# mLSTM gate rows: GpSimd fills the scan's mask, another order of scans and exponential, transposes two ticks later

## The chip, the cores and the metric

The kernel runs on one core of a Trainium2 chip. Its engines are TensorE (PE, with its weight loads, PEld), VectorE (DVE), ScalarE (ACT), GpSimd (POOL) and SyncE, whose queue (SP) issues most DMAs. The metric is the device time of one execution in microseconds; smaller is better. The kernel before takes 2407.82 us (median of three runs, 2406.78 to 2409.0).

## The reference

One inference step of a two-layer encoder, for a prompt of 1024 rows and a sample of 32 rows, all in fp32 with width 1024. Layer 0 is an mLSTM mixer with 4 heads, and an MLP; layer 1 is chunk-band attention and an MLP. The change lies in the mixer, in the two gates of each head:

```
gates = (proj[..., 2 * QK_A + 2 * V_A:] + b_if)
ig = gates[..., :NH_A]
lf = log_sigmoid(gates[..., NH_A:])
# in each chunk:
b = cumsum(lf)                              # restarts at each chunk
dmat = b[t] - b[s] + ig[s]                  # causal, else -inf
m_t = max(b + m, max over s of dmat)        # running maximum
wts = exp(dmat - m_t);  a = exp(b + m - m_t)
h = num / max(abs(den), exp(-m_t))
```

So out of two short rows per head (one value per token) come the sums b, the running maxima m, their differences, and exp(-m), which all later work of the mixer needs, some of it by token along the partitions.

## The kernel before

Tokens are worked on in three blocks of 384, 384 and 288 (TBS). Each fp32 weight and operand is split into a high and a low part (lines 89 and 90: a cast on ScalarE, a subtraction on VectorE), and each product is three matmuls per 128 rows of depth (lines 118 to 120), so a block of a projection is 24 matmuls.

The mixer runs in this order. `v_first` makes the values of head 0 and, in 8 extra columns, the gates, which stand by token along the partitions in `g64`. Then `gate_rows` (lines 526 to 581) works the gates out, and `qk_proj(0, tick)` makes the queries (j = 0) and keys (j = 1) of head 0: three blocks each, a copy of each block by ScalarE (line 600), then on VectorE a convolution of four instructions (lines 608 and 611), and a SiLU in three pieces that goes back and forth between ScalarE (459 to 461, 616) and VectorE (462, 617). For heads 1 to 3, `qk_proj` and `v_proj` follow, and beside them runs `mlstm` of the head before, in steps: `scores` (the product of keys and queries, line 668, and the weights W, line 666), `values` and `heads` (transposes, line 738).

`gate_rows` first turns the gates so that each head is one partition and the tokens lie along the free dimension (transposes, line 542). The rows are 4 partitions by 1056 elements: `ig`, `fr` (forget gate), `tt` (its log-sigmoid, `neglogsig`), `mr` (maxima), `br` (sums) and `rr` (br - mr); br and rr are the two halves of one tile, and `stk` is a tile of 36 partitions, whose first four take ig - br and whose last four take exp(-m). Two scans with add and max make mr (547, 549). A third scan makes br: it multiplies the running value by a mask that is 1, and 0 at each chunk's start, and adds tt. The mask is written into `fr` by two VectorE memsets (551, 552), since fr is no longer needed then. Then come the difference into stk (554), rr (555), its DMA to DRAM, the decay rows (557 to 562) with their DMAs, then -m cut at 80 (569) and its exponential into stk (570), and two small outputs by DMA (571, 572).

At its `yield GATE` the generator stops. It goes on when the flow's ticks have used up GATE: `qk_proj` ticks once after the first and after the second block of the queries, once after their convolution and SiLU, and likewise for the keys. With GATE = 3.0 the rest follows in the program text after the queries' convolution, ahead of the first key block. The rest is nine transposes of stk into `ae_ps` (577), their copies to `ae` (579, 581) and a GpSimd memset (580). `ae` is read by W in `scores`. In between, `ada_l0` (lines 279 and 281) does modulation sums of layer 0 on VectorE in pieces, by ticks too.

The program text isn't the order on the engines. A planner fixes at build time, for each engine, the order in which its instructions stand, from its own estimate of when each is ready, earlier text first among those that are. On the chip each engine then works in that order and waits where an operand is late. So in the trace line 569 stands ahead of line 558 on VectorE. Only the MLPs and the attention have TensorE's order written out.

Of the kernel before, what the change touches and what calls it, by code (L numbers as in the profile page):

```python
# [10 lines left out]
AF = mybir.ActivationFunctionType  # L11
ALU = mybir.AluOpType
# [15 lines left out]
CH = 128  # L28
# [47 lines left out]
def trunk_kernel(ctx: ExitStack, tc: tile.TileContext, a, o):  # L76
    nc = tc.nc
# [101 lines left out]
    def tpt(name):  # L179
        return pa.tile([P, 512], F32, tag="tp", name=name, bufs=2)  # L180
# [269 lines left out]
            pt2[:, 0:16].rearrange("p (q b) -> p q b", q=4)[:, :, :, None].broadcast_to([P, 4, 4, 2]), op=ALU.add)  # L450


    GATE = 3.0
    ADA_C = (2.0, 3.0, 2.0)
    w_in = a["w_in_a"][0]

    def neglogsig(dst, src):

        nc.scalar.activation(dst, src, AF.Abs)
        nc.scalar.activation(dst, dst, AF.Exp, scale=-1.0)  # L460
        nc.scalar.activation(dst, dst, AF.Ln, bias=1.0)
        nc.vector.scalar_tensor_tensor(dst, src, 0.0, dst, op0=ALU.min, op1=ALU.subtract)
# [63 lines left out]
    def gate_rows():  # L526
        nonlocal ae

        def row(name):
            return A.tile([P, YL], F32, tag="y", name=name, bufs=4)[0:NH, :T]  # L530
        ig, fr, tt, mr = row("ig"), row("fr"), row("tt"), row("mr")
        rc = A.tile([P, 2, T], F32, tag="rc", name="rc_rows", bufs=1)
        br, rr = rc[0:NH, 0], rc[0:NH, 1]
        stk = A.tile([P, KC, T], F32, tag="G", name="stk")[0:36, 0]
        nc.gpsimd.memset(stk, 0.0)
        for t0 in range(0, NT, 4):
            ts = list(range(t0, min(NT, t0 + 4)))
            ps = tpt(f"gt_{t0}")
            n = 0
            for t in ts:  # L540
                m = P if t < NT - 1 else TS
                nc.tensor.transpose(ps[:36, n:n + m], g64[:m, t, :], ident[:m, :m])
                n += m
            nc.scalar.activation(ig[:, t0 * P:t0 * P + n], ps[0:NH, :n], AF.Identity, bias=bif[0:4])
            nc.scalar.activation(fr[:, t0 * P:t0 * P + n], ps[32:32 + NH, :n], AF.Identity, bias=bif[32:36])
        neglogsig(tt, fr)
        nc.vector.tensor_tensor_scan(out=mr[:, :TP], data0=tt[:, :TP], data1=ig[:, :TP], initial=0.0,
                                     op0=ALU.add, op1=ALU.max)
        nc.vector.tensor_tensor_scan(out=mr[:, TP:], data0=tt[:, TP:], data1=ig[:, TP:], initial=m0[:, 0:1],
                                     op0=ALU.add, op1=ALU.max)  # L550
        nc.vector.memset(fr, 1.0)
        nc.vector.memset(fr[:, ::CH], 0.0)
        nc.vector.tensor_tensor_scan(out=br, data0=fr, data1=tt, initial=0.0, op0=ALU.mult, op1=ALU.add)
        nc.vector.tensor_sub(stk[0:NH], ig, br)
        nc.vector.tensor_sub(rr, br, mr)
        nc.sync.dma_start(rc_d[0], rr)
        nc.scalar.copy(fr[:, :CH], rr[:, :CH])
        nc.vector.tensor_add(fr[:, CH:TP].rearrange("p (c t) -> p c t", t=CH),
                             rr[:, CH:TP].rearrange("p (c t) -> p c t", t=CH),
                             mr[:, CH - 1:TP - CH:CH][:, :, None].broadcast_to([NH, NCK - 1, CH]))  # L560
        nc.vector.tensor_scalar_add(fr[:, TP:], rr[:, TP:], m0[:, 0:1])
        nc.scalar.activation(fr, fr, AF.Exp)
        nc.sync.dma_start(rc_d[1], fr)
        al = A.tile([NH, NT], F32, name="al")
        nc.vector.tensor_copy(al[:, :NCK], fr[:, CH - 1:TP:CH])
        nc.vector.tensor_copy(al[:, NCK:], fr[:, T - 1:])
        nc.sync.dma_start(al_d, al)
        nc.sync.dma_start(albc, al_d[None].broadcast_to([P, NH, NT]))
        nc.vector.tensor_scalar(tt, mr, -1.0, 80.0, op0=ALU.mult, op1=ALU.min)
        nc.scalar.activation(stk[32:36], tt, AF.Exp)  # L570
        nc.sync.dma_start(o["m_p"].rearrange("a b h -> (a b h)")[:, None], mr[:, TP - 1:TP])
        nc.sync.dma_start(o["m_s"].rearrange("a b h -> (a b h)")[:, None], mr[:, T - 1:T])
        yield GATE
        ps = tpt("ae_ps")
        for t in range(NT):
            m = P if t < NT - 1 else TS
            nc.tensor.transpose(ps[:m, t * 36:(t + 1) * 36], stk[:, t * P:t * P + m], ident[:36, :36])
        ae = A.tile([P, NT, 36], F32, tag="ga", name="ae", bufs=1)
        nc.vector.tensor_copy(ae[:, :NT - 1], ps[:, :(NT - 1) * 36].rearrange("p (t c) -> p t c", c=36))
        nc.gpsimd.memset(ae[:, NT - 1], 0.0)  # L580
        nc.vector.tensor_copy(ae[:TS, NT - 1], ps[:TS, (NT - 1) * 36:NT * 36])
# [221 lines left out]
    for t0, n in TBS:  # L803
        nc.sync.dma_start(xsp[0][:, :, t0:t0 + n], xt[:, :, t0:t0 + n])
    flow.finish()
    gates = flow.add(gate_rows(), now=True)

    def ada_l0():
# [1425 lines left out]
```

## Time and profile before

| what | value |
|---|---|
| median of three runs | 2407.82 us (2406.78 to 2409.0) |
| the profiled execution | 2407.76 us, of which its span is 2405.9 us |
| TensorE busy | 2341.9 us |
| VectorE busy | 1935.6 us |
| ScalarE busy | 1204.7 us |
| GpSimd busy | 168.7 us |
| mean granted clock of TensorE | 0.995 |

A row of the timeline reads: start and duration in us, engine, line, operation, output <- inputs, shape, count, and in square brackets how long the engine had been idle before it and what released it. A row of the waits reads: who, for whom, us in total, times, the longest. A row of busy time by stretch has the stretch, its length, busy us and count of each engine, the granted clock, and the share and rate of the DMA engines. Times are from the start of the span; 1.9 us of the profiled execution lie outside it.

### The profile page before, as it was taken

Reading aid. Unit: us, or ns where it says so; the run is one execution under the profiler, and the core shown is the slowest. Engines: PE = TensorE matmul, PEld = TensorE weight load, DVE = VectorE, ACT = ScalarE, POOL = GpSimd, SP = SyncE. Lnnn points to the kernel's source line nnn. Section 1 sums busy time; section 2 is a strip of 40 time slices with the busy share of each in tenths; the row PEclk is TensorE's granted clock in tenths of the full one; section 3 lists DMA queues with packets and bytes.
Section 4 is the critical chain, followed back from the end, with each engine's and each line's share of the span. In section 5 each row is a group of like instructions: output and inputs, shape, how many; then the busy total and the mean of one; then the engine's idle time right before and its main releaser. Section 6 shows DMA issues by size and latency. Waiting matters only on the chain. (4 is left out here: it accounts for less than half of the span.)

```text
span 2405.9 us, 44188 instructions
## 1 busy us (share of the span) xinstructions
PE 2341.9 (97%) x17180; PEld 2249.5 (93%) x17180; DVE 1935.6 (80%) x3904; ACT 1204.7 (50%) x2452; POOL 168.7 (7%) x322
## 2 busy tenths in 40 slices
PE   7999999999999999999999999999999999899997
PEld 4999999999999999999999987789999999899997
DVE  4888766778788789989888776756998889888777
ACT  4665557278656630101148467773776777222212
POOL 0211100000000000000000224420000000000003
PEclk9999999999999999999999999999999999999999
DMA  8343222526566896675512330051486779976642
GB/s 302 120 137 98 77 91 64 177 93 203 186 197 199 287 341 230 245 268 212 178 61 84 82 93 1 10 140 58 168 278 210 260 280 335 356 257 234 225 148 73
DMA packets 284277, 424.64 MB, mean 177 GB/s; under 512 B 15384, under 2 KB 205228, under 8 KB 278948
## 3 DMA queue, kind: packets, MB, share of 16 engines
q1 hardware_dynamic: 279540, 390.95, 48.3%
q10 hardware_dynamic: 4528, 30.87, 3.2%
q8 instruction: 135, 2.21, 0.4%
q14 instruction: 74, 0.61, 0.1%
HBM read 305.96 MB, written 118.17 MB: 176 GB/s over the span
## 5 line engine op out<-in xcount | busy, mean ns | idle before, releaser
L1133 DVE SCALAR_TENSOR_TENSOR ACX<-dn,ada,ACX 128x264 f32<-128x264 f32 (+6 forms) x664 | 281.7, 447 | 84.3 <-PE dn L1503 41.1
L1503 PE MATMUL dn<-fx,wf_d 128*128 128x264 f32 x2016 | 254.1, 285 | 6.4 <-DVE ACX L1133 4.0
L1503 PEld LDWEIGHTS dn<-fx,wf_d 128*128 128x128 f32 x2016 | 248.8, 188 | 8.7 <-DVE ACX L1133 2.7
L89 ACT CAST w_dn<-raw_dn 128x1024 fp32r<-128x1024 f32 x36 | 37.7, 1051 | 283.3 <-DVE aw L279 124.5
L118 PE MATMUL dn<-hs,w_dn 128*128 128x384 f32 (+2 forms) x512 | 161.3, 315 | 0.0
L119 PE MATMUL dn<-hs,w_dn 128*128 128x384 f32 (+2 forms) x512 | 160.9, 315 | 0.0
L120 PE MATMUL dn<-hs,w_dn 128*128 128x384 f32 (+2 forms) x512 | 156.3, 314 | 1.3 <-DVE w_dn L90 1.3
L1368 PE MATMUL up<-TF,wf_u 128*128 128x264 f32 x1056 | 143.2, 285 | 2.8 <-ACT H L1371 2.8
L1368 PE MATMUL up<-U,wf_u 128*128 128x264 f32 x1056 | 139.8, 285 | 1.1 <-DVE H L1374 0.6
L1368 PE MATMUL up<-u,wf_u 128*128 128x264 f32 x1056 | 139.6, 284 | 1.3 <-ACT wf_u L89 0.7
L279 DVE SCALAR_TENSOR_TENSOR aw<-radw,cs,aw 128x512 f32<-128x512 f32 x196 | 139.5, 743 | 0.8 <-DMA radw<-in_w_ada_dram 0.8
L1368 PEld LDWEIGHTS up<-TF,wf_u 128*128 128x128 f32 x1056 | 134.4, 188 | 3.8 <-ACT H L1371 3.7
L1368 PEld LDWEIGHTS up<-U,wf_u 128*128 128x128 f32 x1056 | 132.9, 188 | 1.9 <-DVE H L1374 1.2
L1368 PEld LDWEIGHTS up<-u,wf_u 128*128 128x128 f32 x1056 | 132.9, 188 | 1.9 <-ACT wf_u L89 0.9
L118 PE MATMUL dn<-U,w_dn 128*128 128x384 f32 (+2 forms) x416 | 129.2, 311 | 0.3 <-DVE ada L304 0.3
L119 PE MATMUL dn<-U,w_dn 128*128 128x384 f32 (+2 forms) x416 | 129.3, 312 | 0.0
L120 PE MATMUL dn<-U,w_dn 128*128 128x384 f32 (+2 forms) x416 | 125.8, 313 | 1.0 <-DVE w_dn L90 0.9
L1876 ACT ACTIVATE p<-p,mx 128x576 f32<-128x576 f32 (+9 forms) x132 | 86.6, 657 | 27.4 <-DVE mx L1873 25.1
L120 PEld LDWEIGHTS dn<-hs,w_dn 128*128 128x128 f32 x512 | 95.9, 188 | 2.0 <-DVE w_dn L90 1.8
L90 DVE TENSOR_TENSOR HL<-H,HL 128x1056 fp32r<-128x1056 f32 x64 | 80.3, 1254 | 21.6 <-ACT HL L89 21.5
L119 PEld LDWEIGHTS dn<-hs,w_dn 128*128 128x128 f32 x512 | 96.4, 188 | 0.0
L118 PEld LDWEIGHTS dn<-hs,w_dn 128*128 128x128 f32 x512 | 96.3, 188 | 0.1
(419 smaller groups left out, 7102.0 us busy)
## 6 DMA issues: line engine op xcount, KB each, us to landing
hpl<-HL SPq DMA_DIRECT2D x144, 264.0 KB
rdn_u<-in_w_up_dram SPq DMA_DIRECT2D x64, 512.0 KB
hd<-HL SPq DMA_DIRECT2D x28, 1056.0 KB
fx<-hd SPq DMA_DIRECT2D x50, 528.0 KB
radw<-in_w_ada_dram SPq DMA_DIRECT2D x24, 1024.0 KB
hd<-HM SPq DMA_DIRECT2D x28, 792.0 KB
raw_up<-in_w_up_dram SPq DMA_DIRECT2D x40, 512.0 KB
raw_dn<-in_w_down_dram SPq DMA_DIRECT2D x36, 512.0 KB
```

What stands on the lines that cost most here:

```text
L89: nc.scalar.copy(dst_h, src)
L90: (eng or nc.vector).tensor_sub(dst_l, src, dst_h.bitcast(F32))
L118: nc.tensor.matmul(ps, wh, mov(0, k), start=(k == 0), stop=False)
L119: nc.tensor.matmul(ps, wh, mov(1, k), start=False, stop=False)
L120: nc.tensor.matmul(ps, wl, mov(0, k), start=False, stop=(k == nk - 1))
L279: nc.vector.scalar_tensor_tensor(acc[cnd], raw[:, k], sc, acc[cnd], op0=ALU.mult, op1=ALU.add)
L1133: nc.vector.scalar_tensor_tensor(xs, ps[:, off + o:off + o + mm_], gate[:, fc, cnd:cnd + 1], xs, op0=ALU.mult, op1=ALU.add)
L1368: nc.tensor.matmul(p, self.ws[w][:, wl, k], moving(f, tp, xl, k), start=first and k + n_ == 0, stop=k == 3 and n_ == 2, skip_group_check=n ...
L1503: nc.tensor.matmul(p, ws[w][:, wl, k], t[:, s0, xl], start=first and k + n_ == 0, stop=k == kg - 1 and n_ == 2, skip_group_check=not first)
L1876: nc.scalar.activation(z, z, AF.Exp, bias=mx[:, 0:1], scale=-1.0, accum_out=mx[:, 1:2])
```

## The change

The mask for the scan of the forget gates is written by two GpSimd memsets into `rr`, which is free until the difference is put there, at the start of `gate_rows`; the two VectorE memsets into `fr` go. The scan into br comes first of the three scans. The cut of -m and its exponential into stk come right behind the scans, ahead of the differences, in place of after the decay rows. GATE is 5.0 in place of 3.0: the transposes stand in the program text after the second key block, ahead of the third.

```
-    GATE = 3.0
+    GATE = 5.0
...
         nc.gpsimd.memset(stk, 0.0)
+        nc.gpsimd.memset(rr, 1.0)
+        nc.gpsimd.memset(rr[:, ::CH], 0.0)
...
         neglogsig(tt, fr)
+        nc.vector.tensor_tensor_scan(out=br, data0=rr, data1=tt, initial=0.0, op0=ALU.mult, op1=ALU.add)
         nc.vector.tensor_tensor_scan(out=mr[:, :TP], data0=tt[:, :TP], data1=ig[:, :TP], initial=0.0,
                                      op0=ALU.add, op1=ALU.max)
         nc.vector.tensor_tensor_scan(out=mr[:, TP:], data0=tt[:, TP:], data1=ig[:, TP:], initial=m0[:, 0:1],
                                      op0=ALU.add, op1=ALU.max)
-        nc.vector.memset(fr, 1.0)
-        nc.vector.memset(fr[:, ::CH], 0.0)
-        nc.vector.tensor_tensor_scan(out=br, data0=fr, data1=tt, initial=0.0, op0=ALU.mult, op1=ALU.add)
+        nc.vector.tensor_scalar(tt, mr, -1.0, 80.0, op0=ALU.mult, op1=ALU.min)
+        nc.scalar.activation(stk[32:36], tt, AF.Exp)
         nc.vector.tensor_sub(stk[0:NH], ig, br)
         nc.vector.tensor_sub(rr, br, mr)
         nc.sync.dma_start(rc_d[0], rr)
...
         nc.sync.dma_start(albc, al_d[None].broadcast_to([P, NH, NT]))
-        nc.vector.tensor_scalar(tt, mr, -1.0, 80.0, op0=ALU.mult, op1=ALU.min)
-        nc.scalar.activation(stk[32:36], tt, AF.Exp)
         nc.sync.dma_start(o["m_p"].rearrange("a b h -> (a b h)")[:, None], mr[:, TP - 1:TP])
```

More of the change, by code (lines that the diff above doesn't have):

```diff
@@ L450, in ada_first @@
             pt2[:, 0:16].rearrange("p (q b) -> p q b", q=4)[:, :, :, None].broadcast_to([P, 4, 4, 2]), op=ALU.add)
-    GATE = 3.0
+    GATE = 5.0
     ADA_C = (2.0, 3.0, 2.0)
@@ L535, in gate_rows @@
         nc.gpsimd.memset(stk, 0.0)
+        nc.gpsimd.memset(rr, 1.0)
+        nc.gpsimd.memset(rr[:, ::CH], 0.0)
         for t0 in range(0, NT, 4):
@@ L546, in gate_rows @@
         neglogsig(tt, fr)
+        nc.vector.tensor_tensor_scan(out=br, data0=rr, data1=tt, initial=0.0, op0=ALU.mult, op1=ALU.add)
         nc.vector.tensor_tensor_scan(out=mr[:, :TP], data0=tt[:, :TP], data1=ig[:, :TP], initial=0.0,
@@ L550, in gate_rows @@
                                      op0=ALU.add, op1=ALU.max)
-        nc.vector.memset(fr, 1.0)
-        nc.vector.memset(fr[:, ::CH], 0.0)
-        nc.vector.tensor_tensor_scan(out=br, data0=fr, data1=tt, initial=0.0, op0=ALU.mult, op1=ALU.add)
+        nc.vector.tensor_scalar(tt, mr, -1.0, 80.0, op0=ALU.mult, op1=ALU.min)
+        nc.scalar.activation(stk[32:36], tt, AF.Exp)
         nc.vector.tensor_sub(stk[0:NH], ig, br)
@@ L568, in gate_rows @@
         nc.sync.dma_start(albc, al_d[None].broadcast_to([P, NH, NT]))
-        nc.vector.tensor_scalar(tt, mr, -1.0, 80.0, op0=ALU.mult, op1=ALU.min)
-        nc.scalar.activation(stk[32:36], tt, AF.Exp)
         nc.sync.dma_start(o["m_p"].rearrange("a b h -> (a b h)")[:, None], mr[:, TP - 1:TP])
```

## The prediction

> **What bounds the kernel now.** I read the page first, then the list of waits of TensorE, then TensorE's order of work around the change, then VectorE, ScalarE and GpSimd over the same stretch.
>
> ```profile
> span 2405.9 us, 44188 instructions
> PE 2341.9 (97%) x17180; PEld 2249.5 (93%) x17180; DVE 1935.6 (80%) x3904; ACT 1204.7 (50%) x2452; POOL 168.7 (7%) x322
> ```
>
> TensorE is busy for 2341.9 of 2405.9 us, so the kernel gains only where TensorE stops waiting or runs faster. The change touches one such place. From the list of TensorE's waits:
>
> ```profile
> PE hT L738 <- ACT hn L731: 3.7, 4, 1.3
> PE ae_ps L577 <- ACT stk L570: 2.4, 1, 2.4
> ```
>
> The nine transposes of the gate rows (L577) wait once, for 2.4 us, for ScalarE's exponential L570. The order on TensorE, first the second key block's start, its last matmul before the wait, and the transposes:
>
> ```profile
> 86.56 0.34 PE L118 MATMUL qk<-U,w_qk 128*128 128x384 f32 x1
> ...
> 89.20 0.33 PE L118 MATMUL qk<-U,w_qk 128*128 128x384 f32 x1
> 91.96 0.72 PE L577 MATMUL ae_ps<-ident,stk 36*128 36x36 f32 x9 [2.43 <-ACT stk L570]
> ```
>
> A block has 8 x 3 = 24 matmuls. From 86.56 to 89.20 at 0.176 us each, 15 have gone by, so the transposes stand behind the sixteenth of the second key block. That is not their place in the program text (ahead of the first key block): the planner that fixes the order at build time put them where its own estimate has the rows ready, and it was about 2.4 us too early.
>
> The wait costs more than its length. Busy time by stretch (columns: length, TensorE, weight loads, VectorE, ScalarE, GpSimd, each with its count, then granted TensorE clock, DMA share, GB/s):
>
> ```profile
> 89.50:92.00 2.50, 0.07 (x2) 0.04 (x1) 2.50 (x5) 1.45 (x3) 0.20 (x2) 1.00 0.05 10
> 92.00:96.00 4.00, 4.00 (x22) 3.94 (x23) 3.92 (x8) 1.86 (x3) 0.68 (x1) 0.64 0.07 12
> 96.00:99.00 3.00, 3.00 (x22) 3.00 (x22) 3.00 (x4) 1.05 (x1) 0.59 (x2) 0.92 0.94 331
> 99.00:113.00 14.00, 14.00 (x87) 14.00 (x87) 12.19 (x18) 10.92 (x30) 3.91 (x7) 1.00 0.17 47
> 113.00:141.00 28.00, 27.72 (x190) 26.30 (x189) 27.93 (x64) 20.08 (x57) 4.24 (x15) 1.00 0.19 61
> ```
>
> Behind the wait the clock is 0.64 for 4 us and 0.92 for 3: 4 x 0.36 + 3 x 0.08 = 1.7 us more. Without the wait TensorE has 2.43 + 1.7 = 4.1 us to gain. The second thing to see is the last row: from 113 to 141 VectorE is busy for 27.93 of 28 us beside a TensorE at 27.72. In that stage two engines run neck and neck.
>
> **Which waits cost the clock.** Three more rows bound it: a wait at the query projection, the stretch behind it, and the stretch that holds the longest wait at the heads, the 1.3 us of the list above:
>
> ```profile
> 1255.86 0.44 PE L120 MATMUL q<-U,w_q 128*128 128x384 f32 x1 [2.88 <-DVE w_q L90]
> ...
> 220.00:225.00 5.00, 4.01 (x27) 2.79 (x28) 1.97 (x7) 3.75 (x11) 0.19 (x2) 1.00 0.57 183
> 1255.00:1260.00 5.00, 4.14 (x16) 4.13 (x17) 5.00 (x7) 0.99 (x2) 0.00 (x0) 0.70 0.51 156
> ```
>
> A wait of 2.88 us is followed by clock 0.70, as the one of 2.43 us by 0.64, while around the 1.3 us the clock stays at 1.00. So the price sets in somewhere between 1.3 and 2.43 us. [...]
>
> **The change part by part.** The gate rows now, on VectorE, then ScalarE, GpSimd and the SP queue, then who uses what follows:
>
> ```profile
> 79.56 2.27 DVE L547 TENSOR_TENSOR_SCAN mr<-tt,ig 4x1024 f32<-4x1024 f32 x1
> 81.76 0.25 DVE L549 TENSOR_TENSOR_SCAN mr<-tt,m,ig 4x32 f32<-4x32 f32 x1
> 82.18 0.94 DVE L551 MEMSET fr<- 4x1056 f32 x1 [0.17 <-issue]
> 83.05 1.15 DVE L90 TENSOR_TENSOR w_qk<-raw_qk,w_qk 128x1024 fp32r<-128x1024 f32 x1
> 84.14 0.73 DVE L279 SCALAR_TENSOR_TENSOR ada_acc<-ada_room,cs,ada_acc 128x512 f32<-128x512 f32 x1
> ...
> 84.80 2.34 DVE L553 TENSOR_TENSOR_SCAN rc_rows<-fr,tt 4x1056 f32<-4x1056 f32 x1
> 87.06 0.72 DVE L279 SCALAR_TENSOR_TENSOR ada_acc<-ada_room,cs,ada_acc 128x512 f32<-128x512 f32 x1
> 87.71 1.24 DVE L554 TENSOR_TENSOR stk<-ig,rc_rows 4x1056 f32<-4x1056 f32 x1
> 88.88 1.24 DVE L555 TENSOR_TENSOR rc_rows<-rc_rows,mr 4x1056 f32<-4x1056 f32 x1
> 90.05 0.69 DVE L569 TENSOR_SCALAR tt<-mr 4x1056 f32<-4x1056 f32 x1
> ...
> 92.71 0.46 DVE L579 COPY ae<-ae_ps 128x288 f32<-128x288 f32 x1
> ...
> 90.82 1.08 ACT L570 ACTIVATE stk<-tt 4x1056 f32<-4x1056 f32 x1 [0.37 <-DVE tt L569]
> ...
> 97.44 1.05 ACT L89 CAST w_v<-raw_v 128x1024 fp32r<-128x1024 f32 x1 [1.77 <-PE qk L120]
> ...
> 104.07 0.97 ACT L666 ACTIVATE W<-rc,ae 128x128 f32<-128x128 f32 x3
> ...
> 66.99 0.97 POOL L535 MEMSET stk<- 36x1056 f32 x1 [20.10 <-DVE w_qk L90]
> ...
> 81.86 0.29 SPq L571 DMA_DIRECT2D out_dram<-mr  x1
> ...
> 84.22 0.40 SPq L96 DMA_DIRECT2D raw_v<-in_w_in_a_dram  x1
> ```
>
> *The mask's memsets leave VectorE.* From the end of L549 (82.01) to L90's start (83.05) that is 1.0 us of a full engine. GpSimd takes over a 4x1056 and a 9-element memset. No row shows them; the nearest is 0.97 us for 36x1056, so about 1.1 us for both, behind the memset at 66.99, done by 69.1. The scan that reads them starts at 79.6 at the earliest: 10 us of cover, cost nothing, and +1.1 us on the chain if that cover were gone. [...]
>
> *The rows are ready earlier.* I keep the three interleaved instructions (1.09 + 0.66 + 0.65 us by their starts). New order from 79.56: scan of the forget gates 2.26, L547 and L549 2.45, the three others 2.4, L569 0.62: it ends at about 87.3. Then the exponential (1.08) and L554 (1.24) run side by side, to about 88.6, against 91.90 now. ScalarE is idle there; behind the exponential in its queue stand only the copies of key blocks.
>
> *The transposes move.* GATE 5.0 puts them behind the second key block's 24 matmuls, which end at 86.56 + 24 x 0.176 = 90.8. The rows are ready 2.2 us before that. The wait goes, unless the planner delays the rows by more than those 2.2 us. Their two copies (L579, 0.46 us, and a short one) and GpSimd's memset of the last row move with them; the first reader is L666 at 104.07, over 10 us later: nothing. L571 and L572 follow L549, now some 2.3 us later, in SP's queue ahead of the load at 84.22; its cast runs at 97.44 and waits for TensorE anyway: nothing.
>
> **Who takes part of it back.** TensorE runs ahead of VectorE by what it gains more. Rows of VectorE, ScalarE, TensorE and the waits of the first head's scores:
>
> ```profile
> 95.79 1.32 DVE L611 SCALAR_TENSOR_TENSOR y<-qkp,pt,y 128x1059 f32<-128x1059 f32 x1
> ...
> 101.38 0.97 DVE L462 SCALAR_TENSOR_TENSOR sl<-y,sl 128x353 f32<-128x353 f32 x2 [1.81 <-ACT sl L461]
> ...
> 112.96 0.95 DVE L617 SCALAR_TENSOR_TENSOR y<-y,sl 128x353 f32<-128x353 f32 x2
> ...
> 99.02 0.37 ACT L600 COPY qkp<-qk 128x256 f32<-128x256 f32 x1 [0.54 <-PE qk L120]
> 99.29 0.89 ACT L459 ACTIVATE sl<-y 128x353 f32<-128x353 f32 x2
> ...
> 113.53 0.49 PE L668 MATMUL S<-y,y 128*128 128x128 f32 x2
> ...
> PEld S L668 <- DVE y L617: 0.5, 1, 0.5
> ...
> 141.22 1.59 ACT L731 ACTIVATE hn<-hn,sm 128x256 f32<-128x256 f32 x3 [0.35 <-DVE sm L727]
> ```
>
> The first scores (L668 at 113.53) already wait for the keys that L617 finishes at 112.96 plus: there is no slack. So their new time is VectorE's. VectorE gains the 1.0 us of memset. It also gains the 1.81 us that it idled at 101.38: ScalarE's L459 was late only because it stood behind the copy L600, and that behind TensorE. With TensorE 4.1 us earlier, L459 can start when the convolution ends (97.1 less 1.0), 3 us earlier, and its result comes before VectorE has done its own work. Together 2.8 us. From there to 141 VectorE has no idle time left to give, and the first heads (L731 at 141.22) hang on it. I therefore take 2.8 us, with 4.1 - 2.8 = 1.3 us of new waiting at L668. The bounds: 4.1 us if the planner sets the scores later, 1.0 us if VectorE keeps its gap.
>
> Sum against the profiled execution, 2407.76 us (1.9 us more than its span): 2407.8 - 2.8 = 2405.0. The median of the runs, 2407.82, is the same to 0.1. Later stages follow TensorE, as its 97% say, so I carry the 2.8 us to the end.
>
> **The rivals.**
> 1. *TensorE keeps all of it.* Order on both engines is planned anew, and scores, set a few matmuls later, find their keys. For it: TensorE has v and key blocks to fill with. Against it: the planner knew nothing of the wait, and sees VectorE's work shorter by the memset, which moves scores earlier if anything. 2407.8 - 4.1 = 2403.7; with heads' waits (3.7 us in all) partly gone too, down to 2400.
> 2. *The wait at L668 costs the clock.* If the scores are planned 1 us earlier, for the shorter VectorE chain, the wait is 1.3 + 1.0 = 2.3 us, next to the 2.43 that cost 1.7. Then 2405.0 + 1.7 = 2406.7.
> 3. *Slower: the heads' transposes L738.* They wait four times, at most 1.3 us, at full clock. Being ahead by 1.3 us there too, TensorE would wait up to 2.6 and pay 1.7 of clock: 3.0 us a head. One head cancels the forecast's gain; two make -2.8 + 6.0 = +3.2, 2411.0. It decides from a wait of about 2.4 us on. Against it: each wait absorbs the lead, so the next head should not find it again.
> 4. *The change doesn't do what it says.* The rows are later than 90.8, because the planner lets convolution or modulation work of VectorE go first. Then the old wait stays and only the memset's 1.0 us is gained: 2406.8.
>
> **How the numbers follow.** Forecast 0.43, rival 1 0.22, rival 2 0.16, rival 3 0.11, rival 4 0.08. The likeliest gives 2405.0. The range goes from the lower part of rival 1, 2401, to a first head lost in rival 3 with some rest, 2409.5; beyond it lie rival 3's two heads and the best of rival 1. A measurement of this kernel can tell about 0.2% from no change, 4.8 us: faster means below 2403.0, slower above 2412.6. Rival 1 only just misses that by its own sum and passes it with one or two head waits less: faster 0.16. Slower needs three heads of rival 3: 0.07. Same 0.77.
>
> **What would show it.** Right: the nine transposes stand behind a whole second key block without a wait, and no stretch between 85 and 105 has a clock below 1.00; the exponential starts near 87.4, beside the subtraction into stk; GpSimd's memsets end before 70; VectorE's gap before L462 near 98 is gone; the first scores start near 110.7 behind a wait of about 1.3 us, at full clock. Wrong: a wait still named at the transposes (rival 4); no new wait at the scores and TensorE 4 us early at 141 (rival 1); a clock below 1.00 behind the scores (rival 2) or behind the heads (rival 3). A time outside 2401 to 2409.5 with these steps in place would mean that the planner moved something far from the gate rows, which no step here covers.

## The result: slower by about 3.4 us

The changed kernel takes 2410.73 us, the median of 22 runs (2407.52 to 2417.05); the kernel before, run beside it, 2407.36 us, the median of 22 (2404.82 to 2411.8). The ratio is 1.0014, 95% interval 1.0008 to 1.0019: slower by about 3.4 us, where 2.8 us less was forecast. By the bound of 0.2% it is no change. The profiled execution of the kernel after took 2410.11 us, 1.8 us more than its span.

First the page of the kernel after, then its list of TensorE's waits (the rows that answer to those of before), each in its own fence:

```profile
span 2408.3 us, 44186 instructions
...
PE 2341.6 (97%) x17180; PEld 2249.8 (93%) x17180; DVE 1932.9 (80%) x3902; ACT 1205.1 (50%) x2452; POOL 168.3 (7%) x324
```

```profile
PE S L668 <- DVE y L617: 4.4, 1, 4.4
PE hT L738 <- ACT hn L731: 4.0, 5, 1.4
```

VectorE's busy time is 2.7 us less, TensorE's the same to 0.3 us, and the span 2.4 us longer. The wait at the transposes (2.4 us) is gone from the list, and one of 4.4 us at the first scores is new. The order on TensorE in the kernel after:

```profile
91.21 0.34 PE L120 MATMUL qk<-U,w_qk 128*128 128x384 f32 x1
91.47 0.72 PE L577 MATMUL ae_ps<-ident,stk 36*128 36x36 f32 x9
...
114.92 0.58 PE L668 MATMUL S<-y,y 128*128 128x128 f32 x1 [4.42 <-DVE y L617]
```

And its busy time by stretch (length, TensorE, weight loads, VectorE, ScalarE, GpSimd, granted clock, DMA share, GB/s):

```profile
85.00:105.00 20.00, 20.00 (x128) 19.69 (x127) 17.94 (x27) 11.11 (x25) 8.04 (x10) 1.00 0.26 85
105.00:110.00 5.00, 5.00 (x35) 5.00 (x34) 5.00 (x5) 0.00 (x0) 0.00 (x0) 1.00 0.43 112
110.00:115.00 5.00, 0.58 (x4) 0.26 (x2) 5.00 (x10) 4.59 (x13) 0.34 (x1) 0.91 0.07 22
115.00:121.00 6.00, 6.00 (x20) 5.63 (x21) 5.23 (x10) 3.00 (x8) 0.29 (x2) 0.50 0.00 0
```

From 85 to 110 TensorE works without a break at clock 1.00, transposes included. Then it waits from 110.5 to 114.92, and behind the wait the clock is 0.50 for 6 us: 6 x 0.5 = 3.0 us more. The new place costs 4.42 + 3.0 = 7.4 us where the old one cost 4.1. The difference, 3.3 us, is close to the 3.4 of the medians. That it fits so well is partly luck: the two profiled spans lie only 2.4 us apart, and the price in clock differs between waits of the same length (last section).

What makes it wait is VectorE. Its rows in the kernel after, from the gate rows to the keys (L617 at 114.35):

```profile
84.80 1.22 DVE L556 TENSOR_TENSOR stk<-ig,rc_rows 4x1056 f32<-4x1056 f32 x1
85.95 0.69 DVE L554 TENSOR_SCALAR tt<-mr 4x1056 f32<-4x1056 f32 x1
...
97.11 0.94 DVE L462 SCALAR_TENSOR_TENSOR sl<-y,sl 128x353 f32<-128x353 f32 x2
97.98 0.73 DVE L279 SCALAR_TENSOR_TENSOR ada_acc<-ada_room,cs,ada_acc 128x512 f32<-128x512 f32 x1
100.53 0.53 DVE L617 SCALAR_TENSOR_TENSOR y<-y,sl 128x353 f32<-128x353 f32 x1 [1.82 <-ACT sl L616]
101.31 0.68 DVE L617 SCALAR_TENSOR_TENSOR y<-y,sl 128x353 f32<-128x353 f32 x1 [0.25 <-ACT sl L616]
...
110.30 2.06 DVE L279 SCALAR_TENSOR_TENSOR ada_acc<-ada_room,cs,ada_acc 128x512 f32<-128x512 f32 x3
112.29 0.69 DVE L288 STREAM_TRANSPOSE ada_room<-ada_acc 128x512 f32<-128x512 f32 x1
...
113.76 0.67 DVE L290 TENSOR_REDUCE cx<-ada_room 128x16 f32<-128x512 f32 x1
114.35 0.94 DVE L617 SCALAR_TENSOR_TENSOR y<-y,sl 128x353 f32<-128x353 f32 x2
```

The pause ahead of L462 is gone (97.11 follows without one). But there is a new one behind it, 1.82 and 0.25 us, and before the keys stand two instructions (L288, L290) that did not stand there. ScalarE over that pause shows what L616 stood behind:

```profile
86.72 1.09 ACT L555 ACTIVATE stk<-tt 4x1056 f32<-4x1056 f32 x1 [1.75 <-DVE tt L554]
...
97.11 0.49 ACT L459 ACTIVATE sl<-y 128x353 f32<-128x353 f32 x1
99.71 0.40 ACT L666 ACTIVATE W<-rc,ae 128x128 f32<-128x128 f32 x1 [2.11 <-POOL rc L645]
100.01 0.49 ACT L616 ACTIVATE sl<-sl 128x353 f32<-128x353 f32 x1
```

The planner has put the first weights W (L666) ahead of the exponential L616. W waits 2.11 us for GpSimd's L645, the causal select in `mlstm` that writes -1e30 into the part of the decay rows that lies in the future. The select of the kernel after, and the one of before:

```profile
95.66 4.18 POOL L645 TENSOR_SCALAR_AFFINE_SELECT rc<-rc 128x1024 f32<-128x1024 f32 x2 [0.58 <-ACT sl L459]
```

```profile
99.61 1.25 POOL L645 TENSOR_SCALAR_AFFINE_SELECT rc<-rc 128x1024 f32<-128x1024 f32 x2
```

Before, the select began at 99.61, just as VectorE had gone idle (99.57 to 101.38), and took 1.25 us. After, it began beside a busy VectorE and took 4.18 us: it ended at 99.84, 1.1 us after VectorE had stopped at 98.71. So the chain of the new pause reads: select slow beside VectorE, W behind the select, L616 behind W in ScalarE's order, VectorE behind L616; and only VectorE's stop seems to let the select through. The experiments test this.

### The profile page after: what moved, and what is told of

Read it like the earlier page. It is cut to its first block, busy times and chain, and to the rows that moved or that the text cites. A ratio compares the mean times of both kernels' runs of the same rounds, so it can differ in the third digit from the quotient of the medians.

```text
span 2408.3 us, 44186 instructions
## 1 busy us (share of the span) xinstructions
PE 2341.6 (97%) x17180; PEld 2249.8 (93%) x17180; DVE 1932.9 (80%) x3902; ACT 1205.1 (50%) x2452; POOL 168.3 (7%) x324
## 5 line engine op out<-in xcount | busy, mean ns | idle before, releaser
L279 DVE SCALAR_TENSOR_TENSOR aw<-radw,cs,aw 128x512 f32<-128x512 f32 x196 | 139.5, 744 | 1.0 <-DMA radw<-in_w_ada_dram 1.0
L90 DVE TENSOR_TENSOR HL<-H,HL 128x1056 fp32r<-128x1056 f32 x64 | 80.2, 1253 | 18.0 <-ACT HL L89 17.9
```

The costliest lines, as they stand in the source:

```text
L90: (eng or nc.vector).tensor_sub(dst_l, src, dst_h.bitcast(F32))
L279: nc.vector.scalar_tensor_tensor(acc[cnd], raw[:, k], sc, acc[cnd], op0=ALU.mult, op1=ALU.add)
```

## The experiments

Each kernel was timed in five rounds against the kernel before on the same chip, whose medians there lay between 2407.8 and 2408.5 us. Two ideas stood against each other at first. The *lead theory*: what counts is how far TensorE is ahead of VectorE when it comes to the first scores. The *order theory*: the new order of the gate rows themselves costs. Later came the *hole theory*: the select needs a pause of VectorE.

**The rows alone, GATE back to 3.0** (rows_only, against the kernel after):

```
-    GATE = 5.0
+    GATE = 3.0
```

> The changed gate rows with GATE back at 3.0. The planned order has the transposes after 16 matmuls of the first key block, the first scores where the changed kernel has them. Lead theory (TensorE's gain at the transposes is only a lead over VectorE, and the first scores wait for VectorE's keys, at a low clock if the wait is over 2.4 us): the rows are ready near 88.6, TensorE is at the transposes near 86, so it waits about 3 us there and runs about 3 us at a low clock; the lead is spent there, the wait at the first scores falls from 4.4 to about 0.5 us, and the time is that of the kernel before, 2407 +- 2. Order theory (the new plan of the rows loses the time wherever the transposes stand): no better than the changed kernel, 2410 or more, with the wait at the scores still over 3 us.

Measured 2408.43 us, ratio 1.0004 (0.9995 to 1.0013). TensorE in this kernel, and two stretches:

```profile
87.57 1.07 PE L577 MATMUL ae_ps<-ident,stk 36*128 36x36 f32 x9 [2.11 <-ACT stk L555]
```

```profile
85.00:90.00 5.00, 2.89 (x16) 2.47 (x15) 5.00 (x7) 1.87 (x3) 0.74 (x2) 0.77 0.03 7
90.00:95.00 5.00, 5.00 (x18) 5.00 (x18) 5.00 (x9) 2.37 (x6) 1.21 (x2) 0.55 0.47 150
```

The transposes are planned earlier, so the rows, though ready earlier, are again too late by 2.11 us (about 3 were expected), and the clock falls, by 5 x 0.23 + 5 x 0.45 = 3.4 us against the 1.7 of before. The scores don't wait. The time can't be told from that of before: the new order of rows by itself shows neither gain nor cost. The order theory, with 2410 or more, falls.

**GATE alone** (gate_only, against the kernel before):

```
-    GATE = 3.0
+    GATE = 5.0
```

> The kernel before with GATE 5.0 alone. Lead theory: the rows are ready at 91.9 as before, the transposes stand behind the second key block at 90.8, so they wait about 1.1 us without loss of clock, TensorE gains 3 us of lead, and the first scores, planned 8 matmuls earlier, wait some 4 us and cost the clock: the time is that of the changed kernel, 2409 to 2411. Order theory (the rows' new order is what costs): the wait at the transposes shrinks, nothing else changes, 2404 to 2405.

Measured 2411.47 us, 1.0014 (1.0005 to 1.0023): the whole loss, and half a us above the lead theory's range. TensorE, then ScalarE, then GpSimd of this kernel:

```profile
93.94 0.72 PE L577 MATMUL ae_ps<-ident,stk 36*128 36x36 f32 x9 [1.01 <-ACT stk L570]
...
114.50 0.63 PE L668 MATMUL S<-y,y 128*128 128x128 f32 x2 [3.46 <-DVE y L617]
```

```profile
105.44 0.40 ACT L666 ACTIVATE W<-rc,ae 128x128 f32<-128x128 f32 x1 [3.11 <-POOL rc L645]
```

```profile
99.63 4.74 POOL L594 COPY qkp<-hist 128x3 f32<-128x3 f32 x1
104.32 1.25 POOL L645 TENSOR_SCALAR_AFFINE_SELECT rc<-rc 128x1024 f32<-128x1024 f32 x2
```

Most of the wait moves from the transposes to the scores, and W stands behind the select here too, for 3.11 us. So it is the step that lets TensorE run ahead that costs; the lead theory holds. The select itself takes only 1.25 us here. It starts late, because a copy of 128x3 ahead of it on GpSimd took 4.74 us beside a busy VectorE (in the kernel after, at 94.89, the same copy took 0.19): it isn't the select as such that VectorE holds up, but what GpSimd happens to be at.

**No select in head 0** (no_select, against the kernel after; the loop over the two selects is empty for h == 0):

```
-        for ap, n in ((rc[:, 0, :TP]...
+        for ap, n in () if h == 0 else ((rc[:, 0, :TP]...
```

> The changed kernel without GpSimd's causal masking of head 0's rows (the two affine_selects of that head are left out, so head 0 isn't causal). All orders stay. Lead theory with the select as VectorE's lost gap: the weights W no longer hold ScalarE for 2.1 us, VectorE's gap of 1.8 us before L617 goes, the keys are ready about 2 us earlier, the wait at the first scores falls from 4.4 to about 2.5 us, and the time by 2 us or, where the clock holds, up to 5: 2406 to 2409. If the select plays no part: the wait stays at 4.4 and the time at 2410.5.

Measured 2407.40 us, 0.9997 (0.9989 to 1.0006), 3.3 us under the kernel after. The first scores and the stretch behind them:

```profile
112.54 0.49 PE L668 MATMUL S<-y,y 128*128 128x128 f32 x2 [2.31 <-DVE y L617]
```

```profile
115.00:121.00 6.00, 6.00 (x37) 5.84 (x36) 6.00 (x11) 2.92 (x9) 0.63 (x4) 1.00 0.00 0
```

VectorE has no pause here and takes 33.21 us from the split at L90 to the keys (78.76 to 111.97), 2.1 us less than in the kernel after (35.32). The wait is 2.1 us shorter too, and the clock stays at 1.00. With two small selects on an engine with 7% of work the whole loss goes.

**The modulation sums later** (ada_later, against the kernel after), to take the two new instructions from the path of the keys:

```
-    flow.add(ada_l0())
+    flow.add(ada_l0(), 7.0)
```

> The changed kernel with the modulation sums of layer 0 started 7 ticks later, so that some 5 us of VectorE's work no longer stand ahead of head 0's keys. Lead theory: the keys are ready 4 to 6 us earlier, the first scores wait under 1 us, no low clock after them, and the time is 7 us below the changed kernel, 2403 to 2405. Order theory (the loss comes from the new order around the rows and not from VectorE being late): 2409 to 2411.

Measured 2411.39 us, 1.0015 (1.0006 to 1.0023): a miss for the lead theory; the order theory, with 2409 to 2411, comes near the time, but rows_only speaks against its cause. Its select and its W:

```profile
97.35 7.01 POOL L645 TENSOR_SCALAR_AFFINE_SELECT rc<-rc 128x1024 f32<-128x1024 f32 x2 [1.04 <-ACT sl L460]
```

```profile
104.23 0.99 ACT L666 ACTIVATE W<-rc,ae 128x128 f32<-128x128 f32 x3 [2.94 <-POOL rc L645]
```

Weight splits (L90) moved into the room of the sums, VectorE stayed busy until 103.2, and the select took 7.01 us and ended at 104.36, again just over 1 us after VectorE had stopped. The run did not isolate the sums, but it made the select's dependence on VectorE plain.

**The select cut into pieces for head 0** (split_h0, against the kernel after): one select of 128x128 for each chunk in place of one of 128x1024, so that the first W needs only the first.

```
+        if h == 0:
+            for c in range(NCK + 1):
+                n = CH if c < NCK else TS
+                ap = rc[:n, 0, c * CH:c * CH + n]
+                nc.gpsimd.affine_select(out=ap, in_=ap, compare_op=ALU.is_ge, fill=-1e30, base=0,
+                                        pattern=[[1, n]], channel_multiplier=-1)
```

> The changed kernel; head 0's causal masking, one affine_select over 8 chunks, is cut into one of 128x128 per chunk. Planned orders of TensorE stay. Hole theory (GpSimd's select gets on only while VectorE pauses, and VectorE pauses only because ScalarE stands behind the weights W, which wait for the whole select): the first piece needs a hole of 0.2 us in place of 1.2, W(0) no longer holds ScalarE, VectorE's gap before L617 falls from 1.8 to under 0.6 us, the first scores wait about 2.5 us in place of 4.4, and the time is that of the run without the select, 2407 to 2408. Rival (a short select has to wait for VectorE's pause just as the long one): gap and wait stay, 2410 to 2411.

Measured 2411.05 us, 1.0012 (1.0004 to 1.0021). The pieces by line (count, shortest, median and longest in ns, first and last start):

```profile
L648 POOL TENSOR_SCALAR_AFFINE_SELECT rc<-rc x9: 289/291/2977, 96.4 to 101.6; 128x128 f32<-128x128 f32 x8, 32x32 f32<-32x32 f32 x1
```

Most pieces take 0.29 us, but one takes 2.98: the first, which met a busy VectorE. W still waited 1.31 us and the scores 4.18. Cutting makes the select shorter, not the time until it gets through: that is what the rival said, and its time came to 0.05 us. The hole theory's time missed; that the select needs a pause shows in the 2977 ns.

**Other orders and pieces.** The scores two units later (scores_u5, against the kernel after):

```
-            if h > 1 or unit[0] >= 3:
+            if h > 1 or unit[0] >= 5:
```

> The changed kernel; head 0's mLSTM steps begin two ticks later, so that TensorE has 29 more matmuls (5 us) ahead of the first scores. Lead theory: no wait at the first scores, no low clock, so the 4.1 us of the old wait are kept: 2403 to 2405. Rival (the later steps of head 0 are pressed together and its heads wait instead): the waits at L738 grow by 3 us or more, 2407 or above.

Measured 2408.73 us, 1.0002 (0.9994 to 1.0011). The scores no longer wait; the list of waits has this in their place:

```profile
PE num L686 <- DVE ct L696: 3.2, 1, 3.2
```

TensorE finds other work ahead of the scores and then waits for VectorE at the values, with a low clock in that stretch (0.83 from 121 to 141, where TensorE is idle for 3.2 us). That is 2 us better than the kernel after, but not better than before, and a miss for the theory, which had 2403 to 2405. The rival had the time (2407 or above) but not the place: the waits at L738 are 3.3 us in all, not more than before. With the select cut in all heads as well (split_all_u5), and with that cut alone in the kernel before (b_split_all):

> Both edits, with the masking cut by chunk in all four heads. Hole theory: as the last run, and the weights of heads 1 to 3 come sooner too (one of them held ScalarE for 3.7 us before): another 0 to 2 us, 2402 to 2405. Rival: same as the run with later steps alone.

> The kernel before with the masking cut by chunk in all four heads. There the first select falls into a gap of VectorE and the first scores don't wait, so head 0 gains nothing; heads 1 to 3 may gain up to the 1.1 to 1.3 us of their waits at L738. Hole theory: 2405 to 2408. Rival (nine short selects cost GpSimd more than one long one): 2408 or more.

Measured 2411.18 us, 1.0012 (1.0004 to 1.0021), and 2411.10 us, 1.0011 (1.0003 to 1.0019). The first is a miss again: the wait of 3.2 us at the values stays, and the heads' transposes now wait up to 2.6 us. In the second the rival had the time: cutting the select costs in the kernel before too, where the heads' transposes wait up to 3.4 us in place of 1.3. That nine short selects cost GpSimd more than one long one, the rival's reason, was not tested by itself.

**Was the pause of the kernel before the select's as well?** (b_nosel: the edit of no_select made in the kernel before.) This tests the reading of before on which the forecast's 1.81 us rest.

> The kernel before without GpSimd's causal selects of head 0 (its scores are then not causal; that part of the computation is left out); the order on TensorE is that of before up to head 0's scores. Narrow theory: in the kernel before, VectorE's pause ahead of the keys' L462 is not the select's doing but comes from ScalarE, whose L459 stands behind the copy L600 and that behind TensorE; it stays at 1.6 to 1.9 us, and the time stays within 2 us of before. Wide theory (each pause of VectorE in this stretch is made by the select): the pause shrinks below 0.4 us, and the keys come 1.5 us earlier; the time stays too, since TensorE, with its wait at the transposes, does not reach the first scores earlier.

Measured 2408.42 us, 1.0001 (0.9992 to 1.0011). VectorE in this kernel:

```profile
101.46 0.96 DVE L462 SCALAR_TENSOR_TENSOR sl<-y,sl 128x353 f32<-128x353 f32 x2 [1.81 <-ACT sl L461]
```

The pause is there to the hundredth, without any select. So before, the select did not make the pause; it slipped into one that was there, which the rows put down to TensorE (through the copy L600). The wide theory falls. After, the pause that TensorE made is gone, and the select makes its own.

**The transposes one block earlier** (gate4: GATE = 4.0 in the kernel after):

> The kernel after with GATE = 4.0: the transposes stand behind one block of the keys (24 matmuls ahead of where they stand in the kernel after), everything else nearly the same. The rows are ready at about 87.8, TensorE is there at about 87.2: a wait of 0.4 to 1.0 us, too short for the clock, so TensorE's lead is smaller by that. Lead theory: the wait at the first scores is 3.4 to 4.0 us and costs the clock as well, 2409.5 to 2411.5. Rival (where the transposes stand counts, not the lead): the wait at the transposes costs the clock, since transposes follow it, and the time is that of before, 2406.5 to 2408.5.

Measured 2410.94 us, 1.0012 (1.0003 to 1.0021). TensorE's two places:

```profile
87.54 0.72 PE L577 MATMUL ae_ps<-ident,stk 36*128 36x36 f32 x9 [0.53 <-ACT stk L555]
...
115.63 0.58 PE L668 MATMUL S<-y,y 128*128 128x128 f32 x1 [4.85 <-DVE y L617]
```

The transposes now wait 0.53 us and lose no clock, the scores wait 4.85 us, and the time is the lead theory's. That the wait grew was outside what the expectation gave (3.4 to 4.0): VectorE paused longer here, 3.49 us ahead of L617. As in gate_only the select ran in 1.25 us, but late: GpSimd's copy L594 of 128x3 ahead of it began at 93.81 beside a busy VectorE and took 7.84 us.

**Head 0's mask on VectorE** (dve_mask, against the kernel after): the triangle is made once at the start, and a minimum puts it on.

```
+    cmask = cp.tile([P, P], mybir.dt.bfloat16, name="cmask")
+    nc.gpsimd.memset(cmask, 1e30)
+    nc.gpsimd.affine_select(out=cmask, in_=cmask, compare_op=ALU.is_ge, fill=-1e30, base=0,
+                            pattern=[[1, P]], channel_multiplier=-1)
...
+            if h == 0:
+                nc.vector.tensor_tensor(out=ap, in0=ap, in1=cmask[:, None, :].broadcast_to([P, NCK, CH]) if n == CH
+                                        else cmask[:TS, :TS], op=ALU.min)
+                continue
```

> The kernel after, with head 0's causal mask put on by VectorE (a minimum with a stored triangle, two instructions, about 1.2 us by L90's row of the same size) in place of GpSimd's selects; nothing is left out. First scores are planned at the 249th matmul in place of the 245th. Theory that the select's pause is what costs: VectorE loses the pause of 1.8 us and gains 1.2 us of work, the keys come 0.7 us earlier, TensorE reaches the scores some 0.6 us later: the wait falls from 4.4 to about 3.1 us and the clock loss with it, 2408 to 2409.5; if the wait falls to 2.3 us or less, no clock loss and 2406 to 2407.5. Rival (VectorE's sum is what counts, the pause is filled by other work): wait 4 us or more, 2410.5 to 2412.

Measured 2406.64 us, 0.9994 (0.9985 to 1.0003). VectorE's mask (its lines stand four further down), TensorE's scores, and the stretch behind them:

```profile
96.49 1.21 DVE L650 TENSOR_TENSOR rc<-rc,cmask 128x1024 f32<-128x1024 f32 x1
```

```profile
113.54 0.49 PE L676 MATMUL S<-y,y 128*128 128x128 f32 x2 [2.31 <-DVE y L621]
```

```profile
115.00:120.00 5.00, 5.00 (x30) 4.89 (x30) 5.00 (x9) 1.63 (x6) 0.10 (x1) 1.00 0.00 0
```

VectorE does 1.2 us more and comes to the last step of the keys 1.35 us sooner (113.00 against 114.35). The wait at the scores is 2.31 us and costs no clock in this execution: the branch of the expectation with 2406 to 2407.5. This is 4.1 us under the kernel after, and the two intervals against the kernel before lie apart. Against the kernel before itself the interval takes in 1: its median is 1.9 us lower, and these runs can't say that it is faster.

**The same mask in the kernel before** (b_dve), to see whether the mask alone does it:

> The kernel before with head 0's mask put on by VectorE as in dve_mask, the gate rows unchanged; nothing is left out. It asks whether the mask by itself makes the kernel faster, or only together with the change to the gate rows. Theory (only together): the wait of 2.4 us at the transposes and its clock stay, VectorE's pause of 1.8 us ahead of the keys' work stays, since TensorE makes it, and 1.3 us of mask come on top: the keys are up to 1.3 us later and the first scores wait as much; 2408 to 2410.5. Rival (the mask alone does it): 2405 to 2407, as dve_mask.

Measured 2407.20 us, 0.9995 (0.9986 to 1.0004). TensorE in this kernel:

```profile
92.42 0.72 PE L581 MATMUL ae_ps<-ident,stk 36*128 36x36 f32 x9 [2.42 <-ACT stk L574]
...
114.25 0.49 PE L676 MATMUL S<-y,y 128*128 128x128 f32 x2 [0.58 <-DVE y L621]
```

The waits are as the theory had them: the old one stays, and the scores wait a little. The time is below its range of 2408 to 2410.5, 0.2 us above the rival's of 2405 to 2407, and can't be told from dve_mask or from before, so the question stays undecided. Whether the change to the gate rows, freed of the select, gains anything of its own stays open too: the two medians lie 0.6 us apart, and each interval reaches about 2 us to either side.

## Why the prediction was wrong

*Right.* The transposes stand behind all 48 key matmuls of two blocks, without a wait and at full clock. The rows were ready before them: the exponential begins at 86.72 and ends at 87.8, 3.7 us ahead of the transposes at 91.47 (it was forecast near 87.4; the instructions that I had kept in between went behind the rows). The memsets went to GpSimd at no cost, though not where the prediction put them, behind the memset at 66.99. In the kernel after, the mask's rows by tile read:

```profile
L536 POOL MEMSET rc_rows<- x1: 967/967/967, 34.3 to 34.3; 4x1056 f32 x1
L537 POOL MEMSET rc_rows<- x1: 208/208/208, 35.4 to 35.4; 4x9 f32 x1
```

That is 1.2 us at 34 us, against an estimate of 1.1. Right, too, was that the first scores are on VectorE's time, and when TensorE would get there. From 113.53 less 4.1, the forecast is 109.4; this profile is 0.6 us later already at the gate rows (L90 at 79.03 against 78.42), and the scores are planned three matmuls further down (0.5 us): 110.5, as measured.

*The step that failed* is "It also gains the 1.81 us that it idled at 101.38". The reading of that pause was right (b_nosel shows it), and it did go. But I took VectorE to have nothing else to pause for. GpSimd's select had used the pause and needs one (1.25 us in it, 4.18 beside VectorE's work); the prediction leaves out who else worked while VectorE stood still. The trace of before had a sign of it: GpSimd's copy L605 of 128x3, which takes 0.19 us at 102.25, took 3.65 at 84.18, beside a VectorE without a pause. From the split at L90 to the keys VectorE took 34.54 us before, and the forecast was 34.54 - 2.8 = 31.7. It took 35.32 (79.03 to 114.35). The memset and the old pause went as forecast. Back came the new pauses, 1.82 + 0.25 = 2.1 us, and one more modulation sum with L288 and L290, which the planner set ahead of the keys, 1.9 us by their starts; about 0.4 us the other way is left over. The share of the pauses is shown by no_select, where VectorE is 2.1 us shorter over the same stretch, and dve_mask bears it out. That of the sums is only counted from the rows, as ada_later did not part it from the rest.

So the term "1.3 us of new waiting at L668" measured 4.42 us, and the clock loss beside it, put at nothing, measured 3.0: together 6.1 us, which is nearly all of the 6.2 between a forecast of -2.8 and a result of +3.4. The 3.0 is that of one execution, so a fit this close is partly luck. What came is the mechanism of rival 2, a wait at the scores that costs the clock, but with 4.4 and 3.0 us in place of 2.3 and 1.7. Its price was capped because it was built on a planner's shift of 1 us, not on VectorE's whole gain failing; by the bound "1.0 us if VectorE keeps its gap" the wait would have been 3.1 us, and the clock's price on that was not worked out. The prediction's reading that the price sets in at a length of wait between 1.3 and 2.43 us does not hold as a rule: the last section has a wait of 2.90 us that cost no clock. Rival 1 (scores planned later) came by 0.5 us only, rival 3 did not come (heads' waits at most 1.4 us), nor rival 4.

## What to carry to other kernels

When a wait of the fast engine goes, the next place where it meets the slow one sets the end; work out both the length and the clock of the wait there, also for the case that the slow engine gains nothing. A pause of an engine is not free time until one has looked at what the other engines do in it: here a GpSimd instruction on nobody's critical path ran in 1.25 us while VectorE stood still, and in 4.18 and 7.01 us where it began beside VectorE's work. If such an instruction has a reader that stands in order ahead of work VectorE needs, it can be worth 1.2 us of VectorE's own time to take it off GpSimd, as it was in the kernel after; in the kernel before, where the select had its pause, the same edit showed no difference.

## What the runs showed of the hardware

**A select on GpSimd beside VectorE.** The same 128x1024 select (with its 32x32 rest) took 1.25 us while VectorE was idle (before, gate_only, gate4), 4.18 and 7.01 us where it began beside a VectorE at work (in the kernel after L279 and L462, in ada_later L90, L462, L279, L617 and L608), and a 128x128 piece took 0.29 or 2.98 us; in the kernel after and in ada_later it ended 1.1 us after VectorE's last instruction before its pause. A copy of 128x3 on GpSimd took 0.19 us or, beside such work, 3.65 (before), 4.74 (gate_only) and 7.84 (gate4). In these rows GpSimd's instruction lasts over several VectorE instructions in a row, and not over one only. It is not always so: in the kernel after, L605 got through in 1.20 us (103.30 to 104.50) at the end of one VectorE instruction (L90, to 104.44), with the next one following at once, and the copy of L605 at 84.61 took 0.19 us beside L552 (84.61 to 84.87). What decides between the two is not shown.

**When a wait costs the clock.** The length of a wait does not settle it. Waits of 2.43 and 2.88 us (before) and of 2.11 (rows_only) were followed by a low clock; waits of 2.31 us (no_select, dve_mask) were not, nor was this one of 2.90 us in the kernel after:

```profile
1258.70 0.45 PE L120 MATMUL q<-U,w_q 128*128 128x384 f32 x1 [2.90 <-DVE w_q L90]
```

What the traces of before and after show is a grid. The clock is 1.00 or 0.50, and the low stretches last 3.41 us or a multiple of it (the last one is cut off by the end). Within a trace they start a whole number of 3.41 us apart: in the kernel before at 93.09 and at 1257.03, which is 341 of them. Busy time in slices of this grid, first before, at the old wait, then after, at the wait of 2.90 us:

```profile
89.67:93.09 3.42, 1.13 (x12) 1.08 (x13) 3.34 (x7) 2.54 (x4) 0.88 (x2) 1.00 0.04 7
93.09:96.50 3.41, 3.41 (x14) 3.41 (x13) 3.41 (x7) 0.77 (x2) 0.00 (x0) 0.50 0.19 43
96.50:99.91 3.41, 3.41 (x26) 3.41 (x25) 3.07 (x4) 1.94 (x4) 1.04 (x4) 1.00 0.79 282
```

```profile
1254.17:1257.59 3.42, 1.63 (x10) 1.31 (x8) 3.36 (x6) 1.76 (x3) 0.00 (x0) 1.00 0.01 2
1257.59:1261.00 3.41, 2.30 (x13) 2.27 (x14) 3.41 (x5) 0.57 (x2) 0.00 (x0) 1.00 0.35 91
```

Before, 2.29 us of idle time fall into one slice, and the next one runs at 0.50. After, the wait is shared between two slices, 1.79 and 1.11 us, and nothing happens. In these two traces, from 45 us on, a slice at full clock with 2.23 us or more of idle time (five of them) was followed by one at 0.50, one with 1.56 or less by one at 1.00, and in between both occur: 1.66 us (after, from 2049.48) led to 0.50, 1.74 (before, from 1260.45) and 1.79 (after, from 1254.17) to 1.00. So a wait of 2 to 3 us costs the clock in one execution and not in the next, depending on where the grid lies, and a low slice costs up to 1.7 us; by these numbers (an estimate, twice 2.23) only a wait of about 4.5 us or more is sure to pay. How long the low clock lasts differs as well: 3.41 us behind a wait of 4.38 (ada_later), 6.83 behind one of 4.42 (after).

It can also stay low for a second slice in which TensorE works throughout. In rows_only TensorE was busy without a break from 87.57 on, but until 88.64 with the nine transposes, and the clock stayed low for a second slice:

```profile
87.69:91.10 3.41, 3.41 (x17) 3.31 (x18) 3.41 (x7) 1.25 (x2) 0.63 (x2) 0.50 0.05 10
91.10:94.52 3.42, 3.42 (x13) 3.42 (x12) 3.42 (x5) 1.30 (x4) 0.73 (x2) 0.50 0.54 167
```

In the kernel before the slice from 93.09 to 96.50, also at 0.50 and just as busy, was followed by one at 1.00. What makes the difference is not shown.
